# A feed-forward quad whose seven products share three PSUM banks, read in between

## The chip, the cores and the metric

One core of one Trainium2 chip. The metric is the device time of one execution of the whole kernel in microseconds; the time before is the median of three runs.

## The reference, cut to what matters

Two layers work on 512 tokens and 256 context tokens of width 1024. Each layer is a feed-forward half-step, a token-mixing part, and a second feed-forward half-step. The change lies in the feed-forward half-steps alone:

```python
def swiglu(h, w_in, w_out):
    gate, up = jnp.split(h @ w_in, 2, axis=-1)
    return (jax.nn.silu(gate) * up) @ w_out

x = x + 0.5 * m(mod_x, 2) * swiglu(modulate(rms_norm(x, g_ffn1), ...), w_ffn1_in, w_ffn1_out)
ctx = ctx + 0.5 * m(mod_c, 2) * swiglu(modulate(rms_norm(ctx, g_ffn1), ...), ...)
```

`w_in` has 2 x 2816 columns, `w_out` 2816 rows. The context is not needed behind the second layer's mixing, so the last feed-forward step works on 512 tokens, and the other three on 768.

## The kernel before, in words

Everything is kept transposed: features on the 128 partitions, tokens along the free dimension. Every fp32 operand of a large product is split into a high and a low fp32r half (`split`, lines 368 to 370: ScalarE copies the high half, another engine subtracts to get the low one), and a product of two operands is three matmuls (`mm3`, line 404: high x high, high x low, low x high).

A feed-forward step (`ffn`) walks through 22 blocks of 128 hidden features in pairs. The first pair is multiplied plainly (`plain`). The other ten pairs are computed by a seven-product scheme that replaces eight block products: for the gate and for the up half there is one `quad` (line 746) each, with the hidden pair as the two output blocks (z = 0, 1) and the tokens cut into two halves t1 and t2 of h = 384 columns (256 in the last step). The seven products are numbered 1 to 7; each contracts 512 features, so it is 4 x 3 = 12 matmuls of 128 x h. Their weights are four operands `w[0]` to `w[3]`, made from raw weights in the stages of `quad_stages`, and their token operands are halves of `hH`/`hL` or the three prepared sums `TH`/`TL` (in the tiles A2, G, A and B, by which the trace's rows tell products 5, 6 and 7). The four outputs are sums of the products:

- z = 0, t1: P1 + P2
- z = 0, t2: P1 + P6 + P5 + P3
- z = 1, t2: P1 + P6 + P7 + P5
- z = 1, t1: P1 + P6 + P7 + P4

A gate output goes through silu; an up output is multiplied by its gate (line 769) and split into a slot, the operand of `down`. Behind the gate quad and the up quad of pair b, `down` (line 813) multiplies the hidden blocks of pair b - 1 by rows of `w_out`: for each of eight output blocks m, 512 tokens and 256 tokens apart, and DVE adds the result into the residual `xT` (line 822). The last `down` covers three blocks and is joined with the next norm.

Before the change each product has its own PSUM bank, handed out by `bank()`: three times out of four a bank from a cycle of four one-bank tiles (`btile`: names g, a, b in the trace), once a `stile` (name s), a tile of two banks of which there are two. The string ORD gives the order of products (digits), copies out of PSUM by ScalarE (c, d), additions by VectorE (u, e, x, y, f, g, h) and weight steps (A). `down` takes a two-bank tile for every other m, one bank for the 512 and one for the 256 tokens.

Weights go through a ring of 1024-column units: eight of them, in the first feed-forward step from the second pair on seven. A quad uses seven units, two each for `w[0]` to `w[2]` and one for `w[3]`. `advance(n)` (line 615) hands n units back and issues the next weight stages as far as units are free: a raw load is issued by SP's queue an item ahead, ScalarE copies the high half, VectorE subtracts the low half. `next(beside)` in each product lets one step of side work (modulation vectors) go along, in the first step only.

What stands on each engine's queue is not the order of the code: at build time a list scheduler reorders every engine's instructions by its own model of when their inputs are ready. Each engine then works strictly in that order. Waits between engines are semaphores that the same build puts in wherever two instructions touch the same tile.

Of the kernel before, what the change touches and what calls it, by code (L numbers as in the profile page):

```python
# [14 lines left out]
AF = mybir.ActivationFunctionType  # L15
ALU = mybir.AluOpType
# [6 lines left out]
SEQ = 512  # L23
# [66 lines left out]
def hybrid_kernel(ctx: ExitStack, tc: tile.TileContext, x, c, ctx_in, c_ctx, w_mod, b_mod, g_ffn1, w_ffn1_in,  # L90
# [3 lines left out]
    nc = tc.nc  # L94
# [4 lines left out]
    pb_ = ctx.enter_context(tc.tile_pool(name="pb", bufs=1, space=PSUM))  # L99
# [15 lines left out]
    reg = {}  # L115
# [18 lines left out]
    def gtile(name="g"):  # L134
        return pg.tile([128, 512], F32, name=name, tag="g")
# [7 lines left out]
    def cyc(*fs):  # L143
        n = [0]

        def f():
            n[0] += 1
            return fs[(n[0] - 1) % len(fs)]()
        return f

    ENG = {"P": nc.gpsimd, "V": nc.vector}
# [4 lines left out]
    def act(dst, src, func, **kw):  # L156

        if table[func] != tabs["set"]:
            ld = nc.scalar.preload_act_table_set(table[func])
            for u in tabs["users"]:  # L160
                tc.add_manual_dep(ld.ins, u.name, order, reason="table")
            tabs.update(set=table[func], load=ld.ins, users=[])
        i = nc.scalar.activation(dst, src, func, **kw).ins  # L163
        tc.add_manual_dep(i, tabs["load"].name, order, reason="table")
        tabs["users"].append(i)
# [7 lines left out]
    def stile(name="s"):  # L173
        return pS.tile([128, 1024], F32, name=name, tag="s")
# [26 lines left out]
    r = 0  # L201
# [12 lines left out]
    ps = gtile()  # L214
# [3 lines left out]
    ps = gtile()  # L218
# [3 lines left out]
    for l in range(DEPTH):  # L222
        ps = gtile()
# [23 lines left out]
    def sum_x(a):  # L247

        sq = P[:, (a % 3) * 1024:(a % 3 + 1) * 1024]
        if CFG["XS"][a] == "V":  # L250
            nc.vector.scalar_tensor_tensor(sq, xin[a], 1.0, xin[a], op0=ALU.mult, op1=ALU.mult, accum_out=ss0[:, a:a + 1])
        else:
            nc.scalar.activation(sq, xin[a], AF.Square, accum_out=ss0[:, a:a + 1])
# [114 lines left out]
    def split(dst_hi, dst_lo, src, lo_eng=None):  # L368
        nc.scalar.activation(dst_hi, src, AF.Copy)  # L369
        (lo_eng or nc.vector).tensor_tensor(dst_lo, src, dst_hi.bitcast(F32), op=ALU.subtract)  # L370
# [6 lines left out]
    def wunit():  # L377
        i = perm[ring[0] % ring[1]]
        ring[0] += 1
        return reg["W%d" % (i // 4)][:, (i % 4) * 1024:(i % 4 + 1) * 1024] if i < 7 else reg["W2"]  # L380

    def wslot():
        return wunit(), wunit()
# [17 lines left out]
    def w_rows(src, r0):  # L401
        return wload(1024, lambda raw: [(raw, src[r0:r0 + 128, :])])

    def mm3(ps, wh, wl, rh, rl, first, last):
        nc.tensor.matmul(ps, wh, rh, start=first, stop=False)  # L405
        nc.tensor.matmul(ps, wh, rl, start=False, stop=False)  # L406
        nc.tensor.matmul(ps, wl, rh, start=False, stop=last)  # L407

    def gemm_steps(ps, w, piece):
        t0, t1 = piece  # L410
# [110 lines left out]
    def ffn(l, which, w_i, w_o, pieces, side=None):  # L521
# [1 line left out]
        slots = {}  # L523
        fi = 2 * l + which
        beside = side() if side else iter(())
        ME, LE, WE, SE, UE = CFG["big" if pieces[-1][1] > SEQ else "small"]
        last = ((0, 256), (256, 512), CP) if CP in pieces else pieces
        h = pieces[-1][1] // 2
        t1, t2 = slice(0, h), slice(h, 2 * h)
# [62 lines left out]
        NPL = 2  # L592
# [16 lines left out]
        def load():  # L609
            if loaded[0] < len(items):  # L610
                raws[loaded[0]] = rawslot(2)
                items[loaded[0]][0](raws[loaded[0]])
                loaded[0] += 1

        def advance(n=0):

            free[0] += n
            while at[0] < len(items):
                i, z = at
                it = items[i]  # L620
                need = 1 if z == 3 and i else 2
                if free[0] < need:
                    return
                free[0] -= need
                if z == 0:
                    while loaded[0] < i + (2 if i else 1) and loaded[0] < len(items):
                        load()
                at[:] = (i, z + 1) if z + 1 < len(it[1]) else (i + 1, 0)
                w = wunit() if need == 1 else wslot()
                it[1][z](raws[i], w)  # L630
                ready.append(w)
                if i == 0 and z == 3:
                    load()

        def slot(j):
            if j not in slots:
                slots[j] = reg["FA" if j % 4 < 2 else "FB"][:, (j % 2) * 1536:(j % 2 + 1) * 1536].rearrange("p (s t) -> p s t", s=2)
            return slots[j]
# [64 lines left out]
        TH, TL = [], []  # L703
# [35 lines left out]
        def tmp():  # L739
            i = tring[0] % 9  # L740
            tring[0] += 1
            return P[:, 1024 + i * 384:1024 + i * 384 + h] if i < 7 else reg["KL"][:, (i - 7) * 384:(i - 7) * 384 + h]

        gates = {}

        def quad(j0, gate):
            w = []

            def prod(wi, u, rh, rl):
                while len(w) <= wi:  # L750
                    w.append(ready.pop(0))
                wh, wl = w[wi] if wi < 3 else (w[3][:, 0:512], w[3][:, 512:1024])
                ps = bank()
                for k in range(4):
                    o = slice(u * 512 + k * 128, u * 512 + (k + 1) * 128)
                    mm3(ps, wh[:, o], wl[:, o], rh[:, k], rl[:, k], k == 0, k == 3)
                next(beside, None)
                return ps

            def put(z, ts, eng, x, y, r):  # L760

                eng.tensor_tensor(r, x, y, op=ALU.add)
                i = 2 * z + (ts is t2)
                if gate:
                    act(r, r, AF.Silu)
                    gates[i] = r
                else:
                    sl = slot(j0 + z)
                    ENG[ME[i]].tensor_tensor(r, r, gates[i], op=ALU.mult)
                    split(sl[:, 0, ts], sl[:, 1, ts], r, ENG[LE[i]])  # L770

            p1, p5, u2, u4 = [tmp() for _ in range(4)]
            ps, freed = {}, [2, 2, 2, 1]
            ops = {
                "1": (0, 0, reg["hH"][:, 0:4, t1], reg["hL"][:, 0:4, t1]), "6": (1, 1, TH[1], TL[1]),
                "2": (0, 1, reg["hH"][:, 4:8, t1], reg["hL"][:, 4:8, t1]), "5": (1, 0, TH[0], TL[0]),
                "3": (2, 0, reg["hH"][:, 4:8, t2], reg["hL"][:, 4:8, t2]), "7": (2, 1, TH[2], TL[2]),
                "4": (3, 0, reg["hH"][:, 0:4, t2], reg["hL"][:, 0:4, t2])}
            for c in CFG["ORD" if j0 > NPL else "ORD1" if gate else "ORD2"]:
                if c in ops:  # L780
                    ps[c] = prod(*ops[c])
                elif c == "c":
                    nc.scalar.activation(p1, ps["1"], AF.Copy)
                elif c == "u":
                    nc.vector.tensor_tensor(u2, p1, ps["6"], op=ALU.add)
                elif c == "e":
                    put(0, t1, nc.vector, p1, ps["2"], p1)
                elif c == "d":
                    nc.scalar.activation(p5, ps["5"], AF.Copy)
                elif c == "x":  # L790
                    ENG[UE[0]].tensor_tensor(u4, u2, p5, op=ALU.add)
                elif c == "y":
                    nc.vector.tensor_tensor(u2, u2, ps["7"], op=ALU.add)
                elif c == "f":
                    put(1, t2, ENG[UE[1]], u2, p5, p5)
                elif c == "g":
                    put(0, t2, nc.vector, u4, ps["3"], u4)
                elif c == "h":
                    put(1, t1, nc.vector, u2, ps["4"], u2)
                else:  # L800
                    advance(freed.pop(0))

        btile = cyc(gtile, atile, btile_, atile)

        qb = [0]

        def bank():
            qb[0] += 1
            return (btile if CFG["QB"][qb[0] % len(CFG["QB"])] == "b" else stile)()[:, :h]

        DM = CFG["DM"]

# [839 lines left out]
    def norm_x(hf):  # L1652
        if not hf:
            h_area()
        for piece in (XP, CP):
            run(norm_apply(0, 0, piece, rb[:, piece[0]:piece[1]], range(4 * hf, 4 * hf + 4)))

    first = {"q": lambda: [sum_x(a) for a in range(6)], "x": load_x, "d": loads, "r": rstd_x, "m": mods0,
             "l": lambda: [lam_setup(l) for l in range(DEPTH)], "s": lambda: half_split(0), "n": lambda: norm_x(0),
             "M": lambda: mods1[0](), "S": lambda: half_split(1), "N": lambda: norm_x(1)}  # L1660
# [6 lines left out]
    for l in range(DEPTH):  # L1667
# [19 lines left out]
        first, last = gla_proj(l, cq)  # L1687
# [25 lines left out]
        last = sparts[G3:] + gparts  # L1713
# [44 lines left out]
```

## Time and profile before

| | |
|---|---|
| three runs | 3041.77 us median (3039.4 to 3048.18) |
| the profiled execution | 3044.36 us, span 3042.6 us |
| granted TensorE clock, mean | 0.984 of 2.4 GHz |
| busy: PE, DVE, ACT, POOL | 2882.5, 2223.7, 1222.9, 501.7 us |

The page is read from the engine shares to the table of stretches and from there to the waits. Four stretches hold the quads and are called stages 1 to 4 below: 120 to 605 us (layer 0, first step), 1215 to 1670 us (layer 0, second), 1768 to 2225 us (layer 1, first) and 2710 to 3000 us (layer 1, second, with 256 columns). PE is TensorE, DVE VectorE, ACT ScalarE. Matmuls overlap, so the step from one start to the next tells more than a matmul's own duration.

### The profile page before, as it was taken

What the parts mean: (1) busy time and instruction counts of PE and PEld (TensorE: products, weight loads), DVE (VectorE), ACT (ScalarE), POOL (GpSimd) and SP (SyncE); (2) the same over time, 40 slices, a digit from 0 to 9 for tenths busy, and PEclk for the clock granted to TensorE, in tenths of its full rate; (3) what the DMA queues carried; (4) which work ended last, traced back from release to release, by engine and by line L of the source; (5) the groups of instructions that cost most, each with busy time, mean ns of one, the idle gap of its engine ahead of it and who ended that gap; (6) DMA issues with size and microseconds to landing.
All of it is one profiled execution on the core that took longest, in us unless ns stands there. A gap on an engine that the chain in (4) does not pass through costs nothing. (4 is left out here: it accounts for less than half of the span.)

```text
span 3042.6 us, 48615 instructions
## 1 busy us (share of the span) xinstructions
PE 2882.5 (95%) x19464; PEld 2505.7 (82%) x19464; DVE 2223.7 (73%) x3881; ACT 1222.9 (40%) x2310; POOL 501.7 (16%) x484
## 2 busy tenths in 40 slices
PE   6999999999999888999999989999999999889998
PEld 4788889988776567989999889999888866679998
DVE  6767677655668877777776687776664679799996
ACT  4332323344455435323323533323253556354443
POOL 3001010110002433011010311010110012233432
PEclk8999999999999999999999999999999999999999
DMA  6332212313435341212222112122222333223332
GB/s 214 111 118 83 88 58 64 90 40 92 107 107 178 105 125 29 83 57 70 64 62 70 56 56 70 60 65 72 61 70 70 82 110 122 74 70 105 104 98 91
DMA packets 314246, 262.38 MB, mean 86 GB/s; under 512 B 27529, under 2 KB 290341, under 8 KB 314021
## 3 DMA queue, kind: packets, MB, share of 16 engines
q1 hardware_dynamic: 311712, 255.47, 27.8%
q10 hardware_dynamic: 2308, 3.82, 0.4%
q8 instruction: 153, 2.51, 0.3%
q14 instruction: 73, 0.59, 0.1%
HBM read 247.72 MB, written 2.10 MB: 82 GB/s over the span
## 5 line engine op out<-in xcount | busy, mean ns | idle before, releaser
L369 ACT ACTIVATE W0r<-R 128x1024 fp32r<-128x1024 f32 (+2 forms) x229 | 219.7, 965 | 384.7 <-PE a L407 84.6
L370 DVE TENSOR_TENSOR W0r<-R,W0r 128x1024 fp32r<-128x1024 f32 (+1 forms) x193 | 216.1, 1124 | 58.2 <-ACT W0r L369 29.8
L822 DVE SCALAR_TENSOR_TENSOR X<-s,dmod,X 128x512 f32<-128x512 f32 x252 | 158.9, 630 | 134.5 <-PE s L407 134.1
L369 ACT ACTIVATE W1r<-R 128x1024 fp32r<-128x1024 f32 (+1 forms) x149 | 141.7, 952 | 270.9 <-PE a L406 87.6
L370 POOL TENSOR_TENSOR FAr<-P,FAr 128x384 fp32r<-128x384 f32 (+2 forms) x68 | 80.8, 1192 | 597.8 <-ACT FAr L369 563.1
L370 POOL TENSOR_TENSOR FBr<-P,FBr 128x384 fp32r<-128x384 f32 (+1 forms) x60 | 70.5, 1177 | 549.4 <-ACT FBr L369 442.2
L163 ACT ACTIVATE P<-s,sm 128x768 f32<-128x768 f32 (+3 forms) x160 | 119.0, 750 | 59.1 <-DVE sm L1053 36.7
L405 PE MATMUL g<-Hr,W0r 128*128 128x384 f32 (+3 forms) x384 | 135.8, 354 | 1.6 <-ACT P L163 1.5
L406 PE MATMUL g<-Hr,W0r 128*128 128x384 f32 (+3 forms) x384 | 132.0, 344 | 0.0
L370 DVE TENSOR_TENSOR W1r<-R,W1r 128x1024 fp32r<-128x1024 f32 (+1 forms) x102 | 110.2, 1087 | 24.7 <-ACT W1r L369 11.4
L822 DVE SCALAR_TENSOR_TENSOR X<-a,dmod,X 128x256 f32<-128x256 f32 (+1 forms) x170 | 101.8, 599 | 23.3 <-PE a L407 22.9
L556 DVE TENSOR_TENSOR P<-R 128x512 f32<-128x512 f32 x80 | 58.9, 736 | 75.2 <-DMA R<-in_w_ffn_in_dram 75.2
L407 PE MATMUL g<-Hr,W0r 128*128 128x512 f32 (+3 forms) x308 | 108.2, 351 | 1.4 <-DVE W0r L370 1.4
L405 PE MATMUL s<-Hr,W0r 128*128 128x256 f32 (+2 forms) x272 | 91.2, 335 | 12.1 <-ACT P L163 7.1
L407 PE MATMUL a<-Hr,W0r 128*128 128x384 f32 (+2 forms) x308 | 100.0, 325 | 0.0
L1053 DVE TENSOR_REDUCE sm<-s 128x1 f32<-128x768 f32 (+1 forms) x80 | 65.8, 844 | 41.2 <-PE s L1052 41.1
L405 PE MATMUL s<-Hr,W1r 128*128 128x256 f32 (+2 forms) x240 | 78.1, 325 | 15.5 <-ACT P L163 12.8
L406 PE MATMUL s<-Hr,W0r 128*128 128x256 f32 (+2 forms) x272 | 89.7, 330 | 2.5 <-POOL Hr L370 1.7
L407 PE MATMUL s<-Hr,W0r 128*128 128x384 f32 (+2 forms) x264 | 86.5, 328 | 0.0
L370 POOL TENSOR_TENSOR Hr<-P,Hr 128x256 fp32r<-128x256 f32 (+1 forms) x64 | 55.6, 871 | 185.3 <-ACT Hr L369 185.0
L405 PE MATMUL a<-Hr,W0r 128*128 128x384 f32 (+2 forms) x256 | 84.7, 331 | 1.2 <-DVE ms L330 1.2
L405 PE MATMUL b<-Hr,W0r 128*128 128x256 f32 (+3 forms) x256 | 85.1, 333 | 0.8 <-ACT FAf L905 0.4
(855 smaller groups left out, 10210.6 us busy)
## 6 DMA issues: line engine op xcount, KB each, us to landing
R<-in_w_ffn_in_dram SPq DMA_DIRECT2D x164, 512.0 KB, 4.0
R<-in_w_mod_dram SPq DMA_DIRECT2D x104, 512.0 KB, 3.9
R<-in_w_ffn_out_dram SPq DMA_DIRECT2D x40, 1024.0 KB, 4.9
R<-in_w_in_dram SPq DMA_DIRECT2D x28, 512.0 KB, 3.9
W2f<-in_w_mod_dram SPq DMA_DIRECT2D x24, 512.0 KB, 3.5
R<-in_w_ffn_in_dram SPq DMA_DIRECT2D x6, 1024.0 KB, 5.9
Gr<-Bf SPq DMA_DIRECT2D x48, 96.0 KB, 2.2
Hf<-in_w_mod_dram SPq DMA_DIRECT2D x4, 1024.0 KB, 12.4
```

What stands on the lines that cost most here:

```text
L163: i = nc.scalar.activation(dst, src, func, **kw).ins
L369: nc.scalar.activation(dst_hi, src, AF.Copy)
L370: (lo_eng or nc.vector).tensor_tensor(dst_lo, src, dst_hi.bitcast(F32), op=ALU.subtract)
L405: nc.tensor.matmul(ps, wh, rh, start=first, stop=False)
L406: nc.tensor.matmul(ps, wh, rl, start=False, stop=False)
L407: nc.tensor.matmul(ps, wl, rh, start=False, stop=last)
L556: ENG[se[0]].tensor_tensor(SB[:, 0:512], a21, a22, op=ALU.add)
L822: nc.vector.scalar_tensor_tensor(xT[:, m, p0:p1], p_, dmod[l][:, 3 + which, m, t:t + 1], xT[:, m, p0:p1], op0=ALU.mult, op1=ALU.add)
L1053: nc.vector.tensor_reduce(sm[:, s:s + 1], S[:, k0:TOK], AX.X, ALU.max, negate=True)
```

## The change

All products of a quad go into three banks: `pa_` and `pc_`, the two banks of one two-bank tile, and `pb_`, a one-bank tile. Product 6 is accumulated onto 1 in `pa_`, then 7 and then 4; product 3 onto 5 in `pc_`; product 2 has `pb_`. Between the accumulations ScalarE copies `pa_` after products 1 and 6 and `pc_` after 5 (three copies for two), and VectorE adds `pb_` after 2, `pa_` after 7 and `pc_` after 3 to those copies (three additions for seven). After product 4 the gate's silu or the up multiplication reads `pa_` itself. The order of products is the same in all quads, 1 2 6 5 7 3 4, where it was 1 6 2 5 3 7 4 or near it, and the four weight steps stand behind 2, 5, 3 and 4.

```diff
-    def mm3(ps, wh, wl, rh, rl, first, last):
+    def mm3(ps, wh, wl, rh, rl, first, last, onto=False):
...
-            def prod(wi, u, rh, rl):
+            S = stile()
+            pa_, pc_, pb_ = S[:, 0:h], S[:, 512:512 + h], btile()[:, :h]
+
+            def prod(wi, u, rh, rl, ps, first=True):
...
-                ps = bank()
                 for k in range(4):
                     o = slice(u * 512 + k * 128, u * 512 + (k + 1) * 128)
-                    mm3(ps, wh[:, o], wl[:, o], rh[:, k], rl[:, k], k == 0, k == 3)
+                    mm3(ps, wh[:, o], wl[:, o], rh[:, k], rl[:, k], first and k == 0, k == 3, not first)
...
-            def put(z, ts, eng, x, y, r):
-                eng.tensor_tensor(r, x, y, op=ALU.add)
+            def put(z, ts, r, x):
                 i = 2 * z + (ts is t2)
                 if gate:
-                    act(r, r, AF.Silu)
+                    act(r, x, AF.Silu)
                     gates[i] = r
                 else:
                     sl = slot(j0 + z)
-                    ENG[ME[i]].tensor_tensor(r, r, gates[i], op=ALU.mult)
+                    (nc.vector if x is not r else ENG[ME[i]]).tensor_tensor(r, x, gates[i], op=ALU.mult)
                     split(sl[:, 0, ts], sl[:, 1, ts], r, ENG[LE[i]])
...
+            def add(r, x):
+                nc.vector.tensor_tensor(r, r, x, op=ALU.add)
+            p1, p5, u2, c21 = [tmp() for _ in range(4)]
+            prod(0, 0, hH[:, 0:4, t1], hL[:, 0:4, t1], pa_)
+            nc.scalar.activation(p1, pa_, AF.Copy)
+            prod(0, 1, hH[:, 4:8, t1], hL[:, 4:8, t1], pb_)
+            add(p1, pb_)
+            put(0, t1, p1, p1)
+            advance(freed.pop(0))
+            prod(1, 1, TH[1], TL[1], pa_, False)
+            nc.scalar.activation(u2, pa_, AF.Copy)
+            prod(1, 0, TH[0], TL[0], pc_)
+            nc.scalar.activation(p5, pc_, AF.Copy)
+            advance(freed.pop(0))
+            prod(2, 1, TH[2], TL[2], pa_, False)
+            add(p5, pa_)
+            put(1, t2, p5, p5)
+            prod(2, 0, hH[:, 4:8, t2], hL[:, 4:8, t2], pc_, False)
+            add(u2, pc_)
+            put(0, t2, u2, u2)
+            advance(freed.pop(0))
+            prod(3, 0, hH[:, 0:4, t2], hL[:, 0:4, t2], pa_, False)
+            put(1, t1, c21, pa_)
+            advance(freed.pop(0))
```

How the build orders it shows at three places, in the sixth quad pair of stage 2. In the changed kernel's rows the lines are shifted: 406 to 408 are the matmuls of `mm3`, 771 the multiplication of `put`, 775 `add`, 781, 787 and 789 the copies p1, u2 and p5.

On PE in the gate quad, before: product 2 (token operand Hr) ends and product 5 (A2r) begins, each in a tile of its own.

```order
L405 MATMUL b_12650<-Hr_9899,W0r_162 128x384
L406 MATMUL b_12650<-Hr_9899,W0r_162 128x384
L407 MATMUL b_12650<-Hr_9899,W0r_162 128x384
L405 MATMUL a_12668<-A2r_10451,W1r_9900 128x384 [waits DVE_49]
L406 MATMUL a_12668<-A2r_10451,W1r_9900 128x384
L407 MATMUL a_12668<-A2r_10451,W1r_9900 128x384
```

And now, where product 6 (Gr) ends and product 5 begins, both in the tile s_12382; s_12491 is the next quad's.

```order
L406 MATMUL s_12382<-Gr_10292,W1r_9740 128x384
L407 MATMUL s_12382<-Gr_10292,W1r_9740 128x384
L408 MATMUL s_12382<-Gr_10292,W1r_9740 128x384
L406 MATMUL s_12491<-Hr_9739,W0r_162 128x384 [waits DVE_49]
L407 MATMUL s_12491<-Hr_9739,W0r_162 128x384
L408 MATMUL s_12491<-Hr_9739,W0r_162 128x384 [waits DVE_49]
L406 MATMUL s_12491<-Hr_9739,W0r_162 128x384
L406 MATMUL s_12382<-A2r_10291,W1r_9740 128x384 [waits Activation_49]
L407 MATMUL s_12382<-A2r_10291,W1r_9740 128x384
```

Four matmuls of the next quad's product 1 now stand between, and product 5 has a wait on ScalarE. Products 7, 3 and 4 have such places too, with the last two waiting on VectorE; in a quad that a `down` follows, matmuls of that `down` stand there.

On ACT in the up quad, before: the copy p1 (783), a weight copy, the copy p5 (789), a slot's high half, a weight copy.

```order
L783 ACTIVATE KLf_10455<-b_12739 128x384 [waits PE_49]
L369 ACTIVATE W0r_162<-R_75 128x1024 [waits PE_49]
L789 ACTIVATE P_74<-g_12788 128x384 [waits PE_49,Pool_49]
L369 ACTIVATE FAr_9940<-KLf_10455 128x384 [waits DVE_49]
L369 ACTIVATE W1r_9900<-R_75 128x1024 [waits DMAHW6_49]
```

And now: silu from PSUM for the gate quad's last output, two weight copies, a slot's high half, then the copies u2 and p5 of the up quad's tile.

```order
L163 ACTIVATE KLf_10295<-s_12382 128x384 [waits PE_49]
L369 ACTIVATE W0r_162<-R_75 128x1024 [waits DMAHW5_49,Activation_49]
L369 ACTIVATE W0r_162<-R_75 128x1024 [waits PE_49]
L369 ACTIVATE FAr_9780<-KLf_10295 128x384 [waits DVE_49]
L787 ACTIVATE P_74<-s_12491 128x384 [waits PE_49,Pool_49]
L789 ACTIVATE P_74<-s_12491 128x384 [waits PE_49]
```

The copy u2 stands behind two weight copies.

On DVE in the gate quad, before: between the weight subtractions (370) stand additions that read tiles of their own.

```order
L762 TENSOR_TENSOR KLf_10455<-KLf_10455,s_12689 128x384 [waits DVE_49,PE_49]
L370 TENSOR_TENSOR W1r_9900<-R_75,W1r_9900 128x1024 [waits PE_49,Activation_49]
L793 TENSOR_TENSOR P_74<-P_74,g_12702 128x384 [waits PE_49]
L370 TENSOR_TENSOR W2r_9901<-R_75,W2r_9901 128x512 [waits Activation_49]
L762 TENSOR_TENSOR P_74<-P_74 128x384 [waits DVE_49]
L762 TENSOR_TENSOR P_74<-P_74,a_12724 128x384 [waits DVE_49,PE_49]
```

And now: the addition after product 7, a weight subtraction, the addition after product 3, a subtraction, then the next quad's first addition and a multiplication.

```order
L775 TENSOR_TENSOR P_74<-P_74,s_12382 128x384 [waits PE_49,Activation_49]
L370 TENSOR_TENSOR W1r_9740<-R_75,W1r_9740 128x1024 [waits PE_49,Activation_49]
L775 TENSOR_TENSOR P_74<-P_74,s_12382 128x384 [waits PE_49]
L370 TENSOR_TENSOR W2r_9741<-R_75,W2r_9741 128x512 [waits Activation_49]
L775 TENSOR_TENSOR KLf_10295<-KLf_10295,a_12492 128x384 [waits PE_49]
L771 TENSOR_TENSOR KLf_10295<-KLf_10295,P_74 128x384 [waits DVE_49]
```

The addition after product 3 stands behind a subtraction that waits for PE.

## Rows read from the trace of the kernel before

**Rows 1.** Page, part 1: busy us (share of span) and instructions by engine.

```profile
PE 2882.5 (95%) x19464; PEld 2505.7 (82%) x19464; DVE 2223.7 (73%) x3881; ACT 1222.9 (40%) x2310; POOL 501.7 (16%) x484
```

**Rows 2.** Stages 1 to 4: us, busy us (count) by engine, PEclk, DMA share, GB/s.

```profile
120.00:605.00 485.00, 462.06 (x2647) 423.29 (x2647) 338.09 (x507) 148.72 (x216) 48.85 (x40) 0.98 0.27 83
1215.00:1670.00 455.00, 445.20 (x2524) 419.09 (x2523) 331.88 (x489) 145.89 (x213) 43.87 (x38) 1.00 0.22 67
1768.00:2225.00 457.00, 444.26 (x2497) 417.39 (x2498) 335.83 (x497) 148.01 (x215) 42.52 (x36) 0.99 0.22 67
2710.00:3000.00 290.00, 287.67 (x2004) 264.09 (x2003) 263.88 (x360) 125.94 (x202) 105.07 (x83) 1.00 0.34 104
```

**Rows 3.** PE's waits on line 822, stages 1 to 4: us in total, times, longest.

```profile
PE s L405 <- DVE X L822: 18.4, 8, 3.7
PE s L405 <- DVE X L822: 9.7, 16, 1.4
PE s L405 <- DVE X L822: 7.8, 15, 1.2
PE s L405 <- DVE X L822: 1.0, 4, 0.4
```

**Rows 4.** PE's timeline, stage 2: start us, us, instruction, count [idle before it].

```profile
1296.90 0.40 PE L405 MATMUL s<-FBr,W0r 128*128 128x512 f32 x1
1298.69 0.39 PE L405 MATMUL s<-FBr,W0r 128*128 128x256 f32 x1 [1.39 <-DVE X L822]
1298.91 0.28 PE L406 MATMUL s<-FBr,W0r 128*128 128x256 f32 x1
```

**Rows 5.** Timeline of DVE at the same place.

```profile
1297.43 0.54 DVE L762 TENSOR_TENSOR P<-P,g 128x384 f32<-128x384 f32 x1
1297.89 0.74 DVE L822 SCALAR_TENSOR_TENSOR X<-s,dmod,X 128x512 f32<-128x512 f32 x1
```

**Rows 6.** As rows 2, by 10 us: behind a long wait, around a shorter one.

```profile
450.00:460.00 10.00, 10.00 (x53) 8.61 (x52) 5.11 (x10) 0.63 (x1) 0.00 (x0) 0.89 0.01 2
1290.00:1300.00 10.00, 8.62 (x49) 7.66 (x48) 9.86 (x14) 3.06 (x5) 3.52 (x3) 1.00 0.30 89
```

**Rows 7.** DVE's busy us over the span, lines 785, 791, 793, 762 alone.

```profile
0.00:3042.60 3042.60, 41.42 (x80) 0.98 0.29 86
0.00:3042.60 3042.60, 57.84 (x80) 0.98 0.29 86
0.00:3042.60 3042.60, 41.14 (x80) 0.98 0.29 86
0.00:3042.60 3042.60, 172.44 (x320) 0.98 0.29 86
```

**Rows 8.** Timeline of PE and ACT, stage 2, 384 columns.

```profile
1314.33 0.34 PE L407 MATMUL a<-Hr,W1r 128*128 128x384 f32 x1
1314.51 0.34 PE L405 MATMUL b<-Gr,W1r 128*128 128x384 f32 x1
1314.77 0.49 ACT L783 ACTIVATE KLf<-a 128x384 f32<-128x384 f32 x1 [0.62 <-PE a L407]
1318.90 1.06 ACT L369 ACTIVATE W1r<-P 128x1024 fp32r<-128x1024 f32 x1 [3.64 <-PE s L407]
```

**Rows 9.** Timeline of PE, ACT and DVE, stage 4, 256 columns.

```profile
2864.53 0.28 PE L407 MATMUL s<-Hr,W0r 128*128 128x256 f32 x1
2864.65 0.28 PE L405 MATMUL a<-Gr,W1r 128*128 128x256 f32 x1
2864.85 0.38 ACT L783 ACTIVATE P<-s 128x256 f32<-128x256 f32 x1 [0.72 <-PE s L407]
2868.70 0.41 DVE L762 TENSOR_TENSOR P<-P,b 128x256 f32<-128x256 f32 x1
```

**Rows 10.** Timeline of DVE, stage 2: a weight subtraction and the addition behind it.

```profile
1318.72 1.23 DVE L370 TENSOR_TENSOR W1r<-R,W0r 128x1024 fp32r<-128x1024 f32 x1 [1.29 <-PE s L406]
1319.87 0.55 DVE L762 TENSOR_TENSOR KLf<-KLf,s 128x384 f32<-128x384 f32 x1
```

More of the change, by code (lines that the diff above doesn't have):

```diff
@@ L402, in w_rows @@
         return wload(1024, lambda raw: [(raw, src[r0:r0 + 128, :])])
-    def mm3(ps, wh, wl, rh, rl, first, last):
-        nc.tensor.matmul(ps, wh, rh, start=first, stop=False)
-        nc.tensor.matmul(ps, wh, rl, start=False, stop=False)
-        nc.tensor.matmul(ps, wl, rh, start=False, stop=last)
+    def mm3(ps, wh, wl, rh, rl, first, last, onto=False):
+        nc.tensor.matmul(ps, wh, rh, start=first, stop=False, skip_group_check=onto)
+        nc.tensor.matmul(ps, wh, rl, start=False, stop=False, skip_group_check=onto)
+        nc.tensor.matmul(ps, wl, rh, start=False, stop=last, skip_group_check=onto)
     def gemm_steps(ps, w, piece):
@@ L525, in ffn @@
         beside = side() if side else iter(())
-        ME, LE, WE, SE, UE = CFG["big" if pieces[-1][1] > SEQ else "small"]
+        ME, LE, WE, SE, _ = CFG["big" if pieces[-1][1] > SEQ else "small"]
         last = ((0, 256), (256, 512), CP) if CP in pieces else pieces
@@ L752, in prod @@
                 wh, wl = w[wi] if wi < 3 else (w[3][:, 0:512], w[3][:, 512:1024])
-                ps = bank()
                 for k in range(4):
                     o = slice(u * 512 + k * 128, u * 512 + (k + 1) * 128)
-                    mm3(ps, wh[:, o], wl[:, o], rh[:, k], rl[:, k], k == 0, k == 3)
+                    mm3(ps, wh[:, o], wl[:, o], rh[:, k], rl[:, k], first and k == 0, k == 3, not first)
                 next(beside, None)
-                return ps
-            def put(z, ts, eng, x, y, r):
-                eng.tensor_tensor(r, x, y, op=ALU.add)
+            def put(z, ts, r, x):
                 i = 2 * z + (ts is t2)
                 if gate:
-                    act(r, r, AF.Silu)
+                    act(r, x, AF.Silu)
                     gates[i] = r
@@ L768, in put @@
                     sl = slot(j0 + z)
-                    ENG[ME[i]].tensor_tensor(r, r, gates[i], op=ALU.mult)
+                    (nc.vector if x is not r else ENG[ME[i]]).tensor_tensor(r, x, gates[i], op=ALU.mult)
                     split(sl[:, 0, ts], sl[:, 1, ts], r, ENG[LE[i]])
[L772 to L801, printed above, removed]
+            def add(r, x):
+                nc.vector.tensor_tensor(r, r, x, op=ALU.add)
@@ new lines, in quad @@
+            p1, p5, u2, c21 = [tmp() for _ in range(4)]
+            freed = [2, 2, 2, 1]
+            hH, hL = reg["hH"], reg["hL"]
+            prod(0, 0, hH[:, 0:4, t1], hL[:, 0:4, t1], pa_)
[6 more added lines that the diff above has]
+            nc.scalar.activation(u2, pa_, AF.Copy)
@@ L803, in ffn @@
+            advance(freed.pop(0))
         btile = cyc(gtile, atile, btile_, atile)
[L805 to L809, printed above, removed]
         DM = CFG["DM"]
```

## The prediction

> **What bounds the kernel now.** I read the page's busy shares first: TensorE (PE) is busy 95% of the span [rows 1]. The change keeps every matmul, so it can move the time only through the gaps between them. Second, the table by stretch, one row for each of the four feed-forward stages [rows 2]: PE is busy 462 of 485 us, 445 of 455, 444 of 457 and 288 of 290, and VectorE (DVE) between 70% and 91%. Third, PE's waits in the same stretches [rows 3]: what PE waits for is DVE's line 822, the read-out of a down product. It waits 18.4 us in 8 waits, then 9.7 in 16, 7.8 in 15 and 1.0 in 4. Fourth, the timeline around such a wait: the quad's last adds hold DVE up [rows 5], so the read-out starts at 1297.89 and ends at 1298.63, and PE, which should have gone on 0.23 us after 1296.90, goes on at 1298.69 [rows 4].
>
> A wait costs more than its recorded idle time. 1296.90 to 1298.91 is 2.01 us [rows 4]; the two spacings without a wait are 0.23 (512 columns, an estimate in proportion to the 0.18 of 384 in [rows 8]) and 0.12 (256 columns [rows 9]). So 1.66 us were lost where 1.39 is recorded: 0.27 more, of which 0.10 is the slow second matmul. In the first stage the granted clock also falls after the longer waits, 0.89 in one 10 us slice; around a 1.39 us wait it stays at 1.00 [rows 6]. Over that stage it is 0.98 of 485 us, 9.7 us.
>
> What the quads and downs lose now: 18.4 + 8 x 0.27 + 9.7 = 30 us in stage 1; 9.7 + 16 x 0.27 = 14 in stage 2; 7.8 + 15 x 0.27 = 12 in stage 3; 2 in stage 4. **58 us is all that a lighter DVE can win.**
>
> **What the change removes.** Per quad the additions u, x, y (lines 785, 791, 793) and one of the four on line 762 go. That is 41.4 + 57.8 + 41.1 + 172.4/4 = 183 us of DVE time over 80 quads [rows 7]. None of it is PE time; it counts only inside the 58 us. One ScalarE (ACT) copy per quad is added, u2, at 0.49 us [rows 8], 36 us in all on an engine that is busy 40% [rows 1]; free, unless it stands behind something. The last product's read, gate or multiply, now takes PSUM directly: the chain from a stage's last quad to its final down is one addition shorter, four times 0.55 [rows 10], about 2 us. Product 2 comes before 6, so the first freeing of weight slots and the side work come one product earlier or later; the loads on SP's queue move by a place or two in stage 1 only. They are issued an item ahead, and I put that at nothing; if a load came late, its DVE stage would wait, not PE. POOL keeps its slot subtractions, in nearly the same order, and no PSUM.
>
> **What the change adds: four round trips per quad.** pa_ and pc_ are two banks of one tile. [Rows 4] show how waits go by tile: the 256-column matmul that writes the second bank of the down's tile waited for DVE's read of the first bank, to 0.06 us after its end. So product 5 into pc_ waits for the copy of pa_ after product 6; 7 waits for the copy of pc_ after 5; 3 for the addition after 7; 4 for the addition after 3. The built order agrees: each has such a wait.
>
> The Trainium skill's page PSUM — Partial Sum Buffer, section "PSUM bank collisions raise a hardware error", asks for guards by bank and quadrant, not by address. By that rule pa_ and pc_ need no wait on one another, the trips vanish, and the sum would be 58 + 2 us less than now. The trace disagrees for this kernel: the wait in [rows 4] is between two banks.
>
> A trip by itself, for 384 columns: 0.44 us from the start of a product's last matmul to the copy, 0.49 copy [rows 8], 0.06 to PE [rows 4, 5], less the 0.18 that follows anyway: 0.81. With DVE's addition of 0.55 [rows 10] it is 0.87. For 256 columns, 0.32 + 0.38 + 0.06 - 0.12 = 0.64 [rows 9], with the 0.41 addition 0.67. Each trip that stops PE at all adds the 0.10 of the slow restart. Uncovered, 320 trips would cost some 290 us. They are covered in part: the built order puts matmuls of the next quad, or of the next down, between.
>
> - **Quad followed by a quad, stages 2 and 3.** Between the products stand 4, 4, 5 and 10 matmuls of 0.18: 0.70, 0.70, 0.87, 1.74. Trips 1 and 2 lose 0.11 + 0.10 each, trip 3 the 0.10. Trip 4's addition stands on DVE behind a weight subtraction of 1.23 us [rows 10] that itself waits for product 3's last reads: 1.23 + 0.55 + about 0.1 is what the ten cover, and I take 0.2. Sum 0.7.
> - **Quad followed by a down.** Covers 1.16, 0.70, 0.93 and 1.9. On ACT the copy of trip 1 stands behind two weight copies of 1.06 [rows 8] and a split: laid out from the end of the quad before, it starts 0.85 late, so 0.81 + 0.85 - 1.16 + 0.10 = 0.6. The others lose 0.2, 0.1, 0.1. Sum 1.0.
> - **The down** still has its two-bank tiles and their waits on DVE: 0.4 where nearly all vanished ones stood at 1.4 or less. A pair: 2.1 to 2.2; twenty pairs, **44 us** against 26.
> - **Stage 1** has one weight slot less, the order differs (covers 0.7, 1.4, 0.9, 0.9, and the addition ahead of the subtraction): 0.6 + 0.85 = 1.5 a pair, ten pairs, **15 us** against 30. No wait comes near those that lowered the clock.
> - **Stage 4**, 256 columns: covers 0.47, 0.47, 0.59, 1.65, then 0.47, 0.70, 0.70, 1.86. Trips lose 0.27, 0.27, 0.2, 0.3; then 0.7 (ACT again), 0.05, 0.1, 0.3. With 0.1 in the down 2.2 a pair, ten pairs, **22 us** against 2.
>
> **Sum:** 81 - 58 - 2 = +21 us on the profiled execution's 3044.4. That execution lies 2.6 us (0.09%) above the median of the runs, 3041.8, so I say **3063**. The bounds: what the counts leave uncovered, with no restart and no queue ahead, is 18 us; and one more weight subtraction ahead of one addition in every second quad is 40 x 1.23 = 49 us on top of 81. I take the middle value since the queue orders were laid out at the durations that the rows show.
>
> **The rivals.**
> - *Faster: the covers suffice and DVE's relief is what remains.* ACT and DVE reach each copy and addition as the product ends, so only 18 us replace 58: 18 - 58 - 2 = -42, 3000 us. It decides at 58/320 = 0.18 us per trip: below it the change wins. For it: DVE loses 183 us of work, the stages' covers are within 0.1 us of the trips. Against: DVE's 0.91 and its 1.23 us subtractions in stage 4. With it I count, at 2 in 100, that the banks do not bind each other after all: 3044.4 - 2.6 - 60 = 2982.
> - *No change:* trips at 0.15 to 0.21 us give back what stage 1 wins, 3033 to 3051.
> - *Much slower: a subtraction gets ahead of the additions.* DVE works strictly in order; in stage 4 it is busy 264 of 290 us. At one in every second quad, 3063 + 49 = 3112.
>
> **How the numbers follow.** My case 42 in 100 (own range 3051 to 3088), faster 23, no change 18, much slower 17. A measurement of this kernel can tell 0.3%, 9 us, from no change. So faster 0.23, same 0.18, slower 0.59. The range from 3012 leaves out the lower half of the faster case and up to 3108 half of the slowest, and takes in both bounds between.
>
> **What would show it.** PE's waits should name ACT's copies and DVE's additions inside quads, some 300 in number, about 0.1 to 0.3 us of recorded idle time each, longest in quads ahead of a down; the waits on line 822's successor should shrink below 15 us, and stage 1's clock should read 0.99 or more. Stage 1 should be some 15 us shorter, stages 2 and 3 together some 18 longer, stage 4 some 20 longer. DVE's total should fall to about 2040 us, ACT's rise to 1260. I am wrong if PE's waits inside quads total under 30 us (faster), or if single waits on the additions exceed 1 us in the last stage (much slower).

## The result, and the profile after

| | before | changed |
|---|---|---|
| median of the runs, us | 3041.28 (3039.40 to 3048.18) | 3080.64 (3078.16 to 3084.64) |
| span of the profiled execution, us | 3042.6 | 3080.8 |

The ratio is 1.0126 with a 95% interval from 1.0106 to 1.0147: 38 us slower, where +21 was forecast, inside the range.

The page's first part answers to [rows 1]:

```profile
PE 2923.9 (95%) x19464; PEld 2495.9 (81%) x19464; DVE 2030.0 (66%) x3561; ACT 1251.7 (41%) x2390; POOL 483.8 (16%) x484
```

DVE fell to 2030 us and ACT rose to 1252, as forecast (2040 and 1260). But PE's busy time rose by 41.4 us, while its idle time fell from 160.1 to 156.9 us (span less busy). The same matmuls are "busy" for longer. How a stop can sit in busy time is shown below.

The table of stretches answers to [rows 2]; columns as there, the last stretch from 2728 us, in which PE was busy 270.86 of the 272 us before:

```profile
120.00:605.00 485.00, 476.61 (x2738) 428.04 (x2740) 292.11 (x441) 160.19 (x244) 47.12 (x40) 0.99 0.29 86
1215.00:1670.00 455.00, 452.63 (x2514) 414.11 (x2514) 282.59 (x405) 151.87 (x229) 41.70 (x37) 1.00 0.21 66
1768.00:2225.00 457.00, 454.94 (x2523) 416.40 (x2522) 286.15 (x412) 153.00 (x231) 40.41 (x37) 1.00 0.23 69
2728.00:3000.00 272.00, 259.18 (x1706) 227.10 (x1707) 188.92 (x245) 113.48 (x190) 81.33 (x71) 0.99 0.30 91
```

Stage 1's clock is 0.99 for 0.98, and DVE has far more room in every stage. Product 5 is the fourth product of a gate quad and of the last up quad in both kernels, so its first matmul is a good milestone. Where it starts in the last up quad of each stage, from PE's timeline, in us:

| | before | changed | difference | forecast, summed up |
|---|---|---|---|---|
| stage 1 | 591.5 | 579.7 | -11.8 | -15 |
| stage 2 | 1676.2 | 1669.2 | -7.0 | -6 |
| stage 3 | 2229.2 | 2225.3 | -3.9 | +3 |
| stage 4 | 3006.1 | 3042.5 | +36.4 | +23 |
| end of the span | 3042.6 | 3080.8 | +38.2 | +21 |

The first gate quad of stage 4 is reached at 2710.1 and 2710.3 us: up to there the two kernels are level in sum. The changed kernel is 6.8 us late at stage 1's first product 5. From a stage's first to its last product 5 it is then 18.6 us shorter in stage 1 and 1.3 and 2.2 us longer in stages 2 and 3, and between the stages it loses 3.5, 0.9 and 4.1 us. Each start is read from one execution: e2, e3 and e4 below, which are the changed kernel up to stage 4, reach stage 3's last product 5 at 2220.3 to 2223.2 us, so 5 us of a difference in the table say little. The 36 us of stage 4 are clear of that, and the net loss arises there. Product 5 of its second and of its ninth gate quad, before and changed, in PE's timelines:

```profile
2743.40 0.28 PE L405 MATMUL a<-A2r,W1r 128*128 128x256 f32 x1
...
2960.00 0.28 PE L405 MATMUL b<-A2r,W0r 128*128 128x256 f32 x1
```

```profile
2746.67 0.39 PE L406 MATMUL s<-A2r,W1r 128*128 128x256 f32 x1
...
2987.83 0.39 PE L406 MATMUL s<-A2r,W0r 128*128 128x256 f32 x1
```

Seven pairs take 216.6 us before and 241.2 now: 30.9 and 34.5 us a pair. In stage 2 the same count gives 47.9 and 47.7.

PE's waits over the whole trace, on the changed kernel's copies and additions, us in total, times, longest:

```profile
PE s L406 <- DVE P L775: 12.7, 19, 1.4
PE s L406 <- ACT P L781: 5.8, 1, 5.8
PE s L406 <- DVE KLf L775: 4.7, 6, 1.1
PE s L406 <- ACT P L789: 1.4, 1, 1.4
PE s L406 <- ACT P L787: 0.6, 1, 0.6
PE s L406 <- ACT KLf L787: 0.2, 1, 0.2
```

That is 29 waits and 25 us, not some 300; those on down's read-out (line 815, the former 822) are gone from the list. The 5.8 us stand ahead of stage 3's first milestone, at 1765.90, where the kernel before waits 5.1 us for a weight copy (line 369); little of them is new. By my own criterion, under 30 us, the kernel should have been faster. The criterion was wrong, as one pair of stage 4 shows on PE's timeline:

```profile
2781.01 0.28 PE L406 MATMUL s<-Hr,W0r 128*128 128x256 f32 x1
2781.31 0.39 PE L406 MATMUL s<-A2r,W1r 128*128 128x256 f32 x1
2781.53 0.28 PE L407 MATMUL s<-A2r,W1r 128*128 128x256 f32 x1
2781.65 0.28 PE L408 MATMUL s<-A2r,W2r 128*128 128x256 f32 x1
...
2796.01 0.28 PE L408 MATMUL s<-Ar,W0r 128*128 128x256 f32 x1
...
2796.70 0.40 PE L407 MATMUL b<-FAr,W0r 128*128 128x512 f32 x1
2798.15 0.38 PE L406 MATMUL s<-Hr,W2r 128*128 128x256 f32 x1 [1.06 <-DVE P L775]
2798.37 0.28 PE L407 MATMUL s<-Hr,W2r 128*128 128x256 f32 x1
...
2801.30 0.40 PE L406 MATMUL s<-FAr,W1r 128*128 128x512 f32 x1
2801.82 0.38 PE L406 MATMUL s<-Hr,W0r 128*128 128x256 f32 x1
```

The first trip of the gate quad stops PE from 2781.01 to 2781.31 and again to 2781.53, where two steps of 0.12 were due: 0.28 us lost, no wait recorded. A 256-column matmul counts as busy for 0.28 us, so a stop of up to 0.16 behind it hides in busy time. Measured from start to start, this pair loses 0.28, 0.28, 0.26 and 0.28 us at the gate quad's four trips (forecast 0.27, 0.27, 0.2, 0.3); 0.6 at the down's first matmul, ahead of the up quad's trip 1 (forecast 0.7, at trip 1; PE's recorded wait there, 0.36 us, is on a weight copy of line 369, which stands ahead of the copy u2 on ACT, and trip 1 itself then loses nothing); 0.1 behind product 7 (forecast 0.05, at trip 2); **1.3 at trip 3** (forecast 0.1); 0.4 at trip 4 (forecast 0.3).

Trip 3 of the up quad is product 3 waiting for the addition behind product 7. DVE's and POOL's timelines there:

```profile
2792.02 1.23 DVE L370 TENSOR_TENSOR W0r<-R,W0r 128x1024 fp32r<-128x1024 f32 x1 [1.74 <-ACT W0r L369]
2794.24 0.69 DVE L557 TENSOR_TENSOR P<-R 128x512 f32<-128x512 f32 x1 [1.00 <-DMA R<-in_w_ffn_in_dram]
2794.85 1.22 DVE L370 TENSOR_TENSOR W1r<-R,W1r 128x1024 fp32r<-128x1024 f32 x1
2795.99 1.78 DVE L558 TENSOR_TENSOR P<-P,R 128x512 f32<-128x512 f32 x1
2797.69 0.41 DVE L775 TENSOR_TENSOR P<-P,s 128x256 f32<-128x256 f32 x1
```

```profile
2795.07 2.15 POOL L559 TENSOR_TENSOR R<-R 128x512 f32<-128x512 f32 x1 [3.52 <-DVE P L557]
```

Product 7's last matmul (operand Ar) starts at 2796.01. The addition, line 775, starts 1.7 us later, since line 558, a sum for the next weights, stands ahead of it and takes 1.78 us beside POOL's sum. The rows above it show why the sums come so late: line 557 waited for a weight load. Eight such waits, 1.05 or 1.06 us each, lie between stage 4's first and last milestones.

Twice in stage 4 the granted clock also fell from 2.4 to 1.2 GHz, just behind waits of 1.05 and 2.4 us, the second in the last pair and for a slot's low half from GpSimd (line 370). The rows, as in [rows 2], give means over 4 us:

```profile
2728.00:2732.00 4.00, 3.81 (x16) 3.52 (x17) 2.54 (x5) 1.47 (x2) 0.78 (x2) 0.59 0.34 102
...
3012.00:3016.00 4.00, 4.00 (x12) 3.10 (x11) 1.49 (x2) 0.00 (x0) 1.09 (x1) 0.57 0.00 0
```

### The profile page after: what moved, and what is told of

Its sections match the earlier page's. It is cut to its first block, busy times and chain, and to the rows that moved or that the text cites. A ratio compares the mean times of both kernels' runs of the same rounds, so it can differ in the third digit from the quotient of the medians.

```text
span 3080.8 us, 48157 instructions
## 1 busy us (share of the span) xinstructions
PE 2923.9 (95%) x19464; PEld 2495.9 (81%) x19464; DVE 2030.0 (66%) x3561; ACT 1251.7 (41%) x2390; POOL 483.8 (16%) x484
## 4 chain that ended last, share of the span: by engine, by line
PE 78%; DVE 13%; DMA 3%; ACT 3%; issue 2%; POOL 1%; DVEq 0%; ACTq 0%; POOLq 0%
PE s L406 13%; PE s L407 12%; PE s L408 12%; PE a L406 3%; PE a L408 3%; PE a L407 3%; PE g L408 3%; PE g L406 3%; PE g L407 3%; PE b L408 2%; PE b L406 2%; PE b L407 2%; DMA R<-in_w_ffn_in_dram 2%; DVE W0r L370 2%; PE b L274 1%
## 5 line engine op out<-in xcount | busy, mean ns | idle before, releaser
L406 PE MATMUL s<-Hr,W0r 128*128 128x384 f32 (+2 forms) x616 | 209.8, 341 | 22.4 <-DVE P L775 8.2
L407 PE MATMUL s<-Hr,W0r 128*128 128x384 f32 (+2 forms) x616 | 201.1, 326 | 2.5 <-POOL Hr L370 1.8
L408 PE MATMUL s<-Hr,W0r 128*128 128x384 f32 (+2 forms) x608 | 197.9, 326 | 1.7 <-DVE W0r L370 1.7
L406 PE MATMUL s<-Hr,W1r 128*128 128x384 f32 (+2 forms) x456 | 154.1, 338 | 17.9 <-ACT P L163 11.6
L370 POOL TENSOR_TENSOR FAr<-P,FAr 128x384 fp32r<-128x384 f32 (+2 forms) x68 | 73.8, 1087 | 614.6 <-ACT FAr L369 543.1
L406 PEld LDWEIGHTS s<-Hr,W0r 128*128 128x128 f32 x616 | 116.9, 190 | 51.4 <-DVE P L775 24.1
L370 POOL TENSOR_TENSOR FBr<-P,FBr 128x384 fp32r<-128x384 f32 (+1 forms) x60 | 63.8, 1065 | 553.4 <-ACT FBr L369 488.0
L407 PE MATMUL s<-Hr,W1r 128*128 128x384 f32 (+2 forms) x456 | 148.3, 325 | 0.0
L408 PE MATMUL s<-Hr,W1r 128*128 128x384 f32 (+2 forms) x448 | 145.0, 324 | 0.2 <-DVE W1r L370 0.2
L775 DVE TENSOR_TENSOR P<-P,s 128x384 f32<-128x384 f32 (+1 forms) x128 | 66.1, 517 | 113.5 <-PE s L408 113.4
L407 PEld LDWEIGHTS s<-Hr,W0r 128*128 128x128 f32 x616 | 117.1, 190 | 6.9 <-POOL Hr L370 2.5
L408 PEld LDWEIGHTS s<-Hr,W0r 128*128 128x128 f32 x608 | 115.1, 189 | 5.7 <-DVE W0r L370 2.6
L406 PEld LDWEIGHTS s<-Hr,W1r 128*128 128x128 f32 x456 | 87.8, 192 | 33.8 <-DVE P L775 12.5
L815 DVE SCALAR_TENSOR_TENSOR X<-a,dmod,X 128x256 f32<-128x256 f32 (+1 forms) x170 | 86.0, 506 | 26.3 <-PE a L408 25.5
L406 PE MATMUL g<-Hr,W0r 128*128 128x512 f32 (+3 forms) x260 | 95.7, 368 | 0.2
```

Source lines behind the costliest of these rows:

```text
L406: nc.tensor.matmul(ps, wh, rh, start=first, stop=False, skip_group_check=onto)
L407: nc.tensor.matmul(ps, wh, rl, start=False, stop=False, skip_group_check=onto)
L408: nc.tensor.matmul(ps, wl, rh, start=False, stop=last, skip_group_check=onto)
L775: nc.vector.tensor_tensor(r, r, x, op=ALU.add)
L815: nc.vector.scalar_tensor_tensor(xT[:, m, p0:p1], p_, dmod[l][:, 3 + which, m, t:t + 1], xT[:, m, p0:p1], op0=ALU.mult, op1=ALU.add)
```

## The experiments

Each row: the median, the ratio to the kernel before, measured beside it, with its interval, and the mean of seven pairs from product 5's starts, as above.

| kernel | median, us | ratio | pair, stage 2 | pair, stage 4 |
|---|---|---|---|---|
| before | | 1 | 47.9 | 30.9 |
| changed | 3080.6 | 1.0126 (1.0106 to 1.0147) | 47.7 | 34.5 |
| e1, pc_ in its own tile | 3026.0 | 0.9937 (0.9924 to 0.9950) | 46.9 | 32.5 |
| e2, the same, stage 4 only | 3052.6 | 1.0029 (1.0018 to 1.0039) | 47.7 | 32.5 |
| e3, changed, sums on DVE | 3069.0 | 1.0081 (1.0065 to 1.0098) | 47.7 | 33.7 |
| e4, changed, sums on POOL | 3074.0 | 1.0096 (1.0080 to 1.0112) | 47.7 | 33.1 |
| e5, e1 with sums on DVE | 3017.4 | 0.9912 (0.9897 to 0.9927) | 46.8 | 32.0 |
| e6, e1 with sums on POOL | 3015.3 | 0.9908 (0.9891 to 0.9925) | 46.8 | 30.7 |
| e7, e1 with down in one-bank tiles | 3011.6 | 0.9892 (0.9876 to 0.9908) | 46.3 | 32.5 |
| e8, before, sums on DVE | 3052.4 | 1.0029 (1.0019 to 1.0039) | 47.8 | 32.0 |
| e9, e6 and e7 together | 2999.5 | 0.9849 (0.9834 to 0.9863) | 46.3 | 30.8 |
| e10, before, order of the change | 3058.6 | 1.0047 (1.0032 to 1.0061) | 48.8 | 31.9 |
| e11, e10 with its sums in place | 3098.1 | 1.0176 (1.0157 to 1.0196) | 49.8 | 32.5 |

**e1: is it the tile?**

```diff
-            pa_, pc_, pb_ = S[:, 0:h], S[:, 512:512 + h], btile()[:, :h]
+            pa_, pb_, pc_ = S[:, 0:h], btile()[:, :h], btile()[:, :h]
```

> The changed kernel in all four steps, but pc_ is a one-bank tile of its own instead of the second bank of pa_'s tile. Same products, order, copies and additions. Theory (the tile ties the banks: a product into one bank waits for the reader of the other): every wait inside a quad now has a whole product of 12 matmuls between, so a 256-column pair goes back from 34.4 to about 31.1 us, the 384-column pairs from 47.6 to 46.5 to 47, and the time to 3015 to 3030 us, faster than both kernels. Rival (the accumulation itself costs: copies and additions stand late in their queues, and each now holds up the next product into its bank): waits on lines 775, 787 and 789 stay, the 256-column pair stays above 33.5 us, the time above 3060.

It took 3026.0 us, 0.6% faster than the kernel before. The arithmetic, the copies and the additions are those of the change; only the second bank lies in a tile of its own. The build then orders the queues anew: in the up quad shown below no matmul of another quad or of the down stands between products 6, 5, 7, 3 and 4 any more. So the tie of the two banks, with what the build makes of it, costs 1.0126 - 0.9937 = 0.0189 of 3043 us, some 57 us, and the rival falls as the cause of the loss. The 384-column pair came out as expected. The 256-column pair did not: 32.5, not 31.1. PE's timeline, and DVE's and POOL's, show what is left there:

```profile
2787.75 0.28 PE L408 MATMUL a<-Hr,W0r 128*128 128x256 f32 x1
2789.55 0.38 PE L406 MATMUL s<-Hr,W0r 128*128 128x256 f32 x1 [1.52 <-DVE P L775]
```

```profile
2786.24 0.69 DVE L558 TENSOR_TENSOR P<-P,R 128x512 f32<-128x512 f32 x1
2786.85 2.31 DVE L370 TENSOR_TENSOR W2r<-R,W1r 128x1024 fp32r<-128x1024 f32 x1
2789.09 0.41 DVE L775 TENSOR_TENSOR P<-P,s 128x256 f32<-128x256 f32 x1
```

```profile
2786.34 1.74 POOL L559 TENSOR_TENSOR R<-R 128x512 f32<-128x512 f32 x1 [0.68 <-DVE P L557]
```

Product 4 goes into the bank that the addition after product 7 must first have read. Even with a whole product between, that addition came late, behind a subtraction of 2.31 us. That is what the rival described, and in stage 4 it stays without the tie.

**e2: where does the tie cost?**

```diff
+            pc_ = btile()[:, :h] if h == 256 else S[:, 512:512 + h]
```

> The changed kernel with pc_ in a tile of its own only in the last step (256 columns). Theory (the loss lies in the last step and is the tie's): a pair of the last step goes from 34.4 to about 31.1 us, its stretch gets 30 to 38 us shorter, the time 3043 to 3051. If the tie costs about as much in the 384-column steps too, the first kernel of this set, without it anywhere, is 15 to 30 us faster than this one; if their pairs are near what the matmuls take, the two agree within 10 us.

3052.6 us, just above the 3043 to 3051 expected, with a pair of 32.5 as in e1. Without the tie in stage 4 the kernel gains 0.0097, some 30 us; without it in the other three another 0.0092, 28 us. I had forecast what quads and downs lose at 22 and 59 us.

**e3 and e4: the addition behind the weight sums.** Of the kernel's line of settings the cut shows one entry, as do those of e7 and e11 below. The four letters are the engines of lines 557 to 560 in stage 4, V for VectorE, P for GpSimd.

```diff
-small=('VPVV', 'PPPP', 'VVVV', 'VVPP', 'VV')
+small=('VPVV', 'PPPP', 'VVVV', 'VVVV', 'VV')
```

> The changed kernel, with the third and fourth of the four weight sums of a quad in the last step on VectorE instead of GpSimd. Theory A (the sum of line 558 ahead of the addition after product 7 is slow because GpSimd works beside it): line 558 goes from about 1.55 to 0.7 us, another sum of 0.7 stands behind it, and the wait before product 3 of the up quads goes from 1.06 to 0.6 to 0.8; the time 3074 to 3080. Theory B (line 558 is slow for a reason of its own): it stays at 1.5, the wait before product 3 grows to 1.7, the time to 3086 to 3092.

> The changed kernel, with all four weight sums of a quad in the last step on GpSimd, so that none stands ahead of the addition after product 7 on VectorE. Theory (that queue position is the term that the forecast had at 0.1 us): the wait of 1.06 us before product 3 of the up quads falls under 0.3, a pair goes from 34.4 to 33.2 to 33.6, the time to 3066 to 3074. Rival (another thing holds the addition, or GpSimd's sums come too late for the weights): the pair stays above 34.

In e4 the fourth string is PPPP. Line 558 over 2740 to 2960 us, in the changed kernel and in e3:

```profile
L558 DVE TENSOR_TENSOR P<-P,R 128x512 f32<-128x512 f32 x13 | 20.1, 1542 | 0.0
```

```profile
L558 DVE TENSOR_TENSOR P<-P,R 128x512 f32<-128x512 f32 x13 | 8.9, 683 | 0.0
```

And PE's waits for the additions in that stretch of e3:

```profile
PE s L406 <- DVE P L775: 2.5, 10, 0.3
...
PE s L406 <- DVE KLf L775: 0.7, 2, 0.3
```

Theory A holds: with none of the sums on POOL this one takes 0.68 us, and though a second one now stands ahead of the addition, the long wait is gone (longest 0.3 us; I had expected 0.6 to 0.8). The kernel gained 0.0045, 14 us, more than expected: 0.7 us in each of the seven pairs, 3.9 and 3.1 in the first and the last. In e4 no sum stands there, the pair fell by 1.4 to 33.1 us, and the longest of the waits in the stretch is 0.3 too; it gained only 0.0030, 9 us (its interval and the changed kernel's overlap a little), since the last pair became longer (45.7 us between the milestones of the last two gate quads, 42.6 in the changed kernel). Together they say that the 1.2 us that the forecast lacked in an up quad came from the weight sum ahead of the addition, slowed by POOL; what else the build moved with these edits is not separated.

**e5 and e6: the same edits without the tie.**

> The kernel with pc_ in a tile of its own (all steps), and the last step's four weight sums all on VectorE. What is left of a pair in the last step is a wait of 1.5 us before product 4 of the gate quad, behind a weight subtraction that took 2.31 us while GpSimd summed, and 1.22 elsewhere. Theory A (GpSimd's sums slow VectorE's work beside them): the subtraction takes 1.2 us, the wait falls to 0.5 or less, the pair from 32.5 to 31.2 to 31.6 us, the time 3013 to 3019 us. Theory B (VectorE simply has too much in this place): with two more sums on it the wait stays or grows, the pair 32.5 or more, the time 3025 or more.

> The kernel with pc_ in a tile of its own, and the last step's four weight sums all on GpSimd. Theory A (GpSimd beside VectorE is what slows it): VectorE has less to do but its subtractions stay slow, 1.5 to 2.3 us, the pair stays at 32 to 33 us, the time at 3020 to 3032. Theory B (too much on VectorE): the wait before product 4 goes, the pair 31.1 to 31.5, the time 3012 to 3017.

e5: the subtraction takes 1.22 us (mean of 7) instead of 1.53, but the wait only falls to 1.0 and the pair to 32.0: half of theory A. A further sum (line 559, 0.69 us) now stands between the subtraction and the addition. e6, over 2740 to 2960 us: the subtraction stays slow, and the waits for the additions are gone:

```profile
L370 DVE TENSOR_TENSOR W2r<-R,W1r 128x1024 fp32r<-128x1024 f32 x7 | 10.9, 1551 | 6.8 <-ACT P L781 4.2 <-PE a L408 1.2 <-PE a L407 0.8
```

```profile
PE s L407 <- POOL FBr L370: 2.6, 1, 2.6
PE s L406 <- ACT FBr L369: 0.2, 1, 0.2
```

The 2.6 us are in the last pair. (The wait in question is before product 4 of the up quad, as a down follows it; the expectation of e5 has it in the gate quad.) In e6's up quad at 2773 us the subtraction still takes 2.12 us right ahead of the addition. But no sum stands before it, so it starts 2.3 us before product 4 is due, where it was 1.0 in e1. What stands ahead of the addition decides; how slow it runs only adds to it. e6's pair, 30.7 us, is even below theory B's, and it took 3015.3 us, as B had it (its first and last pairs are longer). The intervals of e5 and e6 just meet e1's; the pairs, and the waits in them, are clearer than the medians.

**e7: the tie in down.**

```diff
-DM='sbsbsbsb'
+DM='bbbbbbbb'
```

> The kernel with pc_ in a tile of its own, and every read-out pair of down in two one-bank tiles instead of every other one in a two-bank tile. Theory (a tie between the two banks of one tile costs in down what it costs in a quad): the 384-column pair goes from 46.8 to about 46.3 us, 20 to 27 pairs, the time 3012 to 3020. Rival (four banks in turn for all of down are too few, a bank is asked for before it is read out): the pair stays at 46.8 or grows, the time 3026 or more.

3011.6 us, and 46.3 us a pair: the tie costs in down too, 0.5 us a pair and 0.0045, some 14 us, in all, and four banks in turn are enough.

**e8: a control.** The edit of e3 in the kernel before.

> The kernel before, with the last step's four weight sums all on VectorE: a control for the same edit on the changed kernel, which was worth 12 us there. VectorE is busy 91% of that step before the change. If the gain belongs to the changed kernel (its additions stop PE there), this is no faster: 3040 to 3060 us. If taking the sums off GpSimd is a gain whatever the quad does, it is 5 to 12 us faster: 3030 to 3038.

0.3% slower. For the kernel before, the sums were better split than all on VectorE; the change moved the balance.

**e9: together.**

> pc_ in a tile of its own, down's read-out pairs in one-bank tiles, and the last step's four weight sums on GpSimd: the three edits that each gained, together. If they act in different places (the quads, the downs of the 384-column steps, the additions of the last step), their gains add up: a 384-column pair 46.2 us, a 256-column pair 30.7 us, and the time near 3026 - 14 - 11 = 3001 us (2996 to 3006). If two of them remove the same wait, it stays at 3008 to 3012.

2999.5 us, 1.5% faster than the kernel before: the gains add up, as expected.

**e10 and e11: the order of products alone**, in the kernel before, with its own banks and seven additions.

```diff
-ORD='1c6u2eA5dxA37yfAg4hA', ORD1='1c26ueA5dxA37yfAg4hA', ORD2='1c236ueA5dxgA7yfA4hA'
+ORD='1c26ueA5dxA7yf3gA4hA', ORD1='1c26ueA5dxA7yf3gA4hA', ORD2='1c26ueA5dxA7yf3gA4hA'
```

In e10 the strings began 1c2eA6u. There the finished first output, from products 1 and 2, overwrites the copy of product 1 before product 6 is added to it, and so takes that product's place in the other three outputs; the number and size of the operations are the same.

> The kernel before, with its own banks and seven additions, and only the order of the products of the changed kernel: 1 2 6 5 7 3 4, with the weight steps behind 2, 5, 3 and 4. The forecast put the order at nothing. The kernel with pc_ in a tile of its own loses 9 us in the first pair of the first step and 2 to 3 us in the last pair of the 384-column steps against the kernel before. Theory A (the order does that: weight units come free and side work is asked for at other places): the same places are longer here, 62 to 65 us instead of 55.6 in the first pair, 57 to 59 instead of 55.4 in the last, and the time 3050 to 3060 us. Theory B (the shared banks do it): these pairs stay at 55 to 56 us and the time within 9 us of the kernel before.

> The kernel before with the order of products 1 2 6 5 7 3 4, as in the run just made, but with each product's additions as in the kernel before: the sum of products 1 and 6 is formed ahead of the sum of 1 and 2. That run took 3058.6 us. If it is the order of products and weight steps that costs, this one is within 6 us of it, 3052 to 3064. If it was the place of the additions, it is back within 9 us of the kernel before, 3034 to 3052.

e10 was 0.5% slower, within theory A's range, and e11, outside both expectations, 1.8%. So the order is not free, but its price hangs on where the additions stand: 14 us in e10, where the first output is finished ahead of product 6 as in the changed kernel, and 54 in e11. PE's waits in e11, the line that answers to 36.9 us in 43 waits in the whole trace of the kernel before:

```profile
PE s L405 <- DVE X L822: 64.7, 31, 3.3
```

Of theory A's places, stage 1's first pair (60.2 us before) is longer, 63.2 and 67.1, and the last pairs of stages 2 and 3 by 1.1 to 2.7 us; stage 1's last pair is not. The main loss of e11 lies in the pairs between, in stages 2 to 4 (table), and these waits of PE for down's read-outs, 28 us more than before, are half of it. That the additions y, f and g now crowd the end of the quad, ahead of those read-outs on DVE, is how I read it; no run moved them one by one.

## Why the prediction was right, and where its sum was off

**The tile ties the banks: right, and the cause of the loss.** e1 changes nothing but the tile, and with it the order that the build makes, and 57 us go. By the Trainium skill's page PSUM — Partial Sum Buffer, section "PSUM bank collisions raise a hardware error", two banks need no guard against each other. e1 agrees: its copy u2 reads one bank from 2783.86 to 2784.25 us while product 5's matmuls into another go on in steps of 0.12. The waits of the changed kernel come from how the build places semaphores, by tile.

**Stage 4, 22 us against 2: mis-sized.** Its own terms add up to 2.3 us a pair, 23 and not 22. Some 20 us more than before were forecast; between the first and last milestones it measured 36 more (296.0 and 332.1 us). Six of the eight losses in a pair were right to within 0.1 us. A seventh, 0.6 for 0.7, agrees by size alone: PE waited for the weight copy itself and not for the copy behind it. The eighth, trip 3 of the up quad at 0.1, measured 1.3: some 10 us over the eight pairs that have it. The step that failed was to count the addition as ready when its product ends. The rival "a subtraction gets ahead of the additions" came near this mechanism (here it is a weight sum), and its sign, single waits over 1 us in the last stage, is there; but it priced it for every stage, and it came in one. The last pair (42.6 us for 36.3), with the 2.4 us wait for a slot and the fall of the clock behind it, makes most of the rest.

**Stages 2 and 3, 44 us against 26: too much.** PE's steps beyond 0.17, 0.23 and 0.12 us add up to 10.2 us in seven pairs of stage 2, 1.5 a pair and not 2.2, mostly single restarts of 0.11 us: the covers sufficed. The kernel before lost 11.8 in such seven pairs. So a pair in the middle of stage 2 got 0.2 us shorter, not 0.9 longer, and in stage 3 it stayed at 47.7. The last pair of each stage got 1.5 to 2.3 us longer; in stages 2 and 3 that is not the tie's doing alone, since e10, with the old banks, has 1.1 and 1.3 us of it, and e1, without the tie, takes 57.1 and 58.6 us there. From stage 1's last milestone to stage 3's the kernel gave back 7.9 us (3 to 5 in e2, e3 and e4), not 18, and 3.5 of them lie within the quads.

**Stage 1, 15 us shorter: right in size**, 11.8 at its last milestone, the clock at 0.99. Whether the lighter DVE won it is open: e10, with all seven additions, is 10.1 us early there too.

**81 - 58 - 2 = +21: two sizes that were wrong against each other.** Without the tie (e1) the kernel wins 19 us, not 60; the tie costs 57, where I had 81 for all that quads and downs still lose. These make +38, where I had +21. One step that failed on the winning side is the order of products, put at nothing: alone it costs 14 us (e10) or 54 (e11). The chains from a stage's last quad to the next stage, put at 2 us shorter in all, were 10 us longer by the two traces (3.5, 0.9, 4.1, and 1.8 at the end). A few us of that can be the execution's, as said above; no run shows why. The sign was right, partly because the errors offset each other, and that the time lies inside the range is in part luck.

**The way I meant to see it was wrong.** Recorded waits leave out short stops; the sum of steps from start to start, or the pair's period, shows them.

## What to carry to other kernels

When several results share banks, give each bank a tile of its own before judging the idea: here the same change was 1.3% slower with two banks in one tile and 0.6% faster without. Once an addition outside PSUM gates the next product, everything that stands ahead of it on its in-order engine belongs to PE's path, so the side work must be placed anew (sums that were better split over VectorE and GpSimd than all on VectorE were no longer so). Look for short stops in the period of a repeated pattern, not in the list of waits.

## What the runs showed of the hardware

A VectorE sum of two 128x512 operands (line 558) took 0.68 us with GpSimd idle (e3) and 1.54 on average beside GpSimd's sums (the changed kernel), at most 1.78 in the stretch shown. The starts fit taking turns by whole instructions: in e1 line 558 ends at 2786.93 and POOL's sum at 2788.08, and the subtraction of 2.31 us ends 1.08 behind that, about the 1.22 that it takes undisturbed. The Trainium skill, page SBUF — State Buffer, section "SBUF: two separate sides", describes a port pair shared by VectorE and GpSimd, held by one for a whole instruction, while the other is blocked; the rows agree.
